# A log-sum-exp kernel: ScalarE instead of SyncE waits for the last store

## The chip, the cores and the metric

One core of a Trainium2 chip. The time is that of one execution on the device, in microseconds (us), over several executions of each kernel. Traces are of one profiled execution of each kernel. In lines of the profile PE is TensorE, ACT ScalarE, DVE VectorE, POOL GpSimd and SP SyncE; a q behind the name means that the engine's sequencer did it, and L176 is line 176 of the kernel.

## The reference

For x of shape 32 x 512 x 1024 in float32, drawn from a normal distribution, the maximum plus the logarithm of the sum of exponentials over the last axis:

```python
x_max = np.max(x, axis=axis, keepdims=True)
return (x_max.squeeze(axis) + np.log(np.sum(np.exp(x - x_max), axis=axis))).astype(np.float32)
```

The output is 16384 numbers, 64 KB; the input is 67 MB. The kernel leaves the maximum out, which this input allows.

## The kernel before

The 16384 rows lie on 128 partitions, 128 rows each. SyncE streams them in 17 chunks through a ring in the on-chip memory. ScalarE takes exponentials, and sums some rows itself; VectorE sums the rest. ScalarE takes the logarithms, the last one of 4 columns. Then SyncE stores the result and ends the program:

```python
    take_logs(late_row, NB, late[:, : NB - late_row], dves, acts)   # ScalarE's last work
    nc.sync.wait_ge(act_done, acts)
    nc.sync.dma_start(out=out_v, in_=res).then_inc(stored, 16)
    # (cut: blank lines)
    nc.sync.sem_clear(range(used[0], used[-1] + 1))   # the 19 semaphores of the run
    nc.sync.wait_ge(stored, 16)                       # the store has landed
    nc.sync.sem_inc(stored, -16)                      # its semaphore is 0 again
```

The wait and the decrement of `stored` are built into one instruction (the trace has one record of 17 ns for the two lines). The store adds 16 to its semaphore, in 16 updates from 160.984 to 161.161 us, all of them after the last of its packets had begun (160.807). Where this text says that a store or a load has landed, it means its 16th count.

The softmax here doesn't subtract the row's maximum and nothing guards it: scores larger than these inputs give would overflow.

## Time and profile before

| | before |
|---|---|
| time, median of 3 runs | 162.69 us (162.61 to 162.76) |
| span of the profiled execution (first to last instruction of the kernel) | 161.19 us |
| time of that execution | 162.52 us |
| last logarithm ends | 159.59 us |
| store issued by SyncE | 159.62 us |
| store's 16th count arrives | 161.161 us |
| SyncE's last instruction, the wait, ends | 161.194 us |

The lines of the profile behind this table stand in the prediction. In short: 159.6 us of loads, exponentials and sums, 1.6 us of store, and 1.3 us of measured time that lies outside the span. Behind the kernel's last instruction the trace has no instruction of this kernel, only updates of semaphores. Below, "the tail" means that stretch, and "the closing barrier", or "the first barrier", the first group of updates of semaphore 2 that ends in it. The "second barrier" is the group of nine updates that opens 0.79 us after the first one's end; it took 0.358 us, and is the one called undisturbed. A "hop" is the time from one such update to the next, and an engine's "own step" is the time from the end of its last recorded instruction to its first update. "On the way out" names the first five of the nine updates, and "back" the last four. These are names alone.

### The profile page before, as it was taken

What the parts mean: (1) busy time and instruction counts of PE and PEld (TensorE: products, weight loads), DVE (VectorE), ACT (ScalarE), POOL (GpSimd) and SP (SyncE); (2) the same over time, 40 slices, a digit from 0 to 9 for tenths busy, and PEclk for the clock granted to TensorE, in tenths of its full rate; (3) what the DMA queues carried; (4) which work ended last, traced back from release to release, by engine and by line L of the source; (5) the groups of instructions that cost most, each with busy time, mean ns of one, the idle gap of its engine ahead of it and who ended that gap; (6) DMA issues with size and microseconds to landing.
All of it is one profiled execution on the core that took longest, in us unless ns stands there. A gap on an engine that the chain in (4) does not pass through costs nothing.

```text
span 161.2 us, 149 instructions
## 1 busy us (share of the span) xinstructions
DVE 121.0 (75%) x46; ACT 115.1 (71%) x40; POOL 0.2 (0%) x4
## 2 busy tenths in 40 slices
DVE  0028000003999999999999699999999999999892
ACT  3170005996079960999419993999199999999995
POOL 0000000000000000000000000000000000000000
DMA  7999699899899899899889999999899999999990
GB/s 260 504 488 488 290 442 520 374 407 520 374 407 520 374 407 520 374 407 520 374 374 455 455 455 439 423 423 423 385 439 430 434 441 413 418 431 415 409 406 32
DMA packets 2592, 67.18 MB, mean 417 GB/s; under 512 B 288, under 2 KB 416, under 8 KB 928
## 3 DMA queue, kind: packets, MB, share of 16 engines
q1 hardware_dynamic: 2592, 67.18, 97.2%
HBM read 67.11 MB, written 0.07 MB: 417 GB/s over the span
## 4 chain that ended last, share of the span: by engine, by line
DMA 48%; DVE 29%; ACT 20%; issue 0%
DMA ring<-in_x_dram 48%; DVE sums L157 29%; ACT ring L137 17%; ACT ring L164 3%; ACT res L108 0%
## 5 line engine op out<-in xcount | busy, mean ns | idle before, releaser
L157 DVE TENSOR_REDUCE sums<-ring 128x8 f32<-128x8192 f32 (+5 forms) x14 | 111.2, 7994 | 37.1 <-ACT ring L137 37.0
L137 ACT ACTIVATE ring<-ring 128x8192 f32<-128x8192 f32 (+6 forms) x18 | 104.4, 5835 | 43.1 <-DMA ring<-in_x_dram 42.9
L144 DVE CUSTOM_DVE_ANT_0 ring<-ring 128x512 f32<-128x512 f32 x16 | 9.9, 686 | 0.0
L164 ACT ACTIVATE ring<-ring 128x1024 f32<-128x1024 f32 x9 | 9.3, 1042 | 0.0
L122 ACT ACT_TABLE_LOAD x1 | 1.3, 1283 | 1.4 <-PEq L70 1.4
L164 ACT ACTIVATION_READ_ACCUMULATOR ring<-ring 128x1 f32 x9 | 1.6, 174 | 0.0
L144 DVE DVE_READ_ACCUMULATOR2_ANT sums<- 128x1 f32 x16 | 1.3, 83 | 0.0
L108 ACT ACTIVATE res<-sums 128x81 f32<-128x81 f32 (+1 forms) x2 | 0.5, 248 | 0.0
L108 ACT ACTIVATE res<-late 128x4 f32<-128x4 f32 x1 | 0.2, 173 | 0.0
L209 POOL MEMSET const-bfloat16-1.0<- 128x1 bf16 x1 | 0.1, 101 | 0.0
L209 POOL MEMSET const-uint8-127<- 128x1 uint8 x1 | 0.1, 101 | 0.0
L209 POOL MEMSET const-float32-0.0<- 128x1 f32 x1 | 0.1, 98 | 0.2 <-issue 0.2
L209 POOL MEMSET const-float32-1.0<- 128x1 f32 x1 | 0.1, 98 | 0.0
## 6 DMA issues: line engine op xcount, KB each, us to landing
ring<-in_x_dram SPq DMA_DIRECT2D x1, 7680.0 KB, 24.4
ring<-in_x_dram SPq DMA_DIRECT2D x1, 7168.0 KB, 28.6
ring<-in_x_dram SPq DMA_DIRECT2D x1, 6656.0 KB, 35.7
ring<-in_x_dram SPq DMA_DIRECT2D x1, 4608.0 KB, 20.3
ring<-in_x_dram SPq DMA_DIRECT2D x2, 2048.0 KB, 16.0
ring<-in_x_dram SPq DMA_DIRECT2D x1, 3584.0 KB, 28.3
ring<-in_x_dram SPq DMA_DIRECT2D x1, 2560.0 KB, 27.3
ring<-in_x_dram SPq DMA_DIRECT2D x4, 512.0 KB, 27.0
```

The source lines that it names most:

```text
L108: nc.scalar.activation(out=res[:, lo:hi], in_=src, func=Ln).then_inc(act_done, 1)
L122: nc.scalar.preload_act_table_set("natural_log_exp_and_others")
L137: nc.scalar.activation(out=ring[:, s + lo : s + hi], in_=ring[:, s + lo : s + hi], func=Exp).then_inc(act_done, 1)
L144: nc.vector.tensor_tensor_reduce(out=ring[:, s + j, : D // 2], in0=ring[:, s + j, : D // 2], in1=ring[:, s + j, D // 2 :], scale=1.0, scal ...
L157: nc.vector.reduce_sum(out=sums[:, row + lo : row + hi], in_=ring[:, s + lo : s + hi], axis=AX).then_inc(dve_done, 1)
L164: nc.scalar.activation(out=ring[:, s + j], in_=ring[:, s + j], func=Exp, accum_out=total(row + j),).then_inc(act_done, 1)
L209: nc = _bacc.Bacc("TRN2", target_bir_lowering=False, num_devices=1)
```

## The change

The intent seems to be that SyncE, which has issued the store and cleared the semaphores, need not sit until the store has landed; ScalarE, which has nothing left to do, takes the wait.

```diff
@@ -177,8 +178,8 @@
     nc.sync.sem_clear(range(used[0], used[-1] + 1))
-    nc.sync.wait_ge(stored, 16)
-    nc.sync.sem_inc(stored, -16)
+    nc.scalar.wait_ge(stored, 16)
+    nc.scalar.sem_inc(stored, -16)
```

A blank line higher up moves all later line numbers by one: L176 of before is L177 of the changed kernel.

## The prediction

One of the limits of "the four ways", 163.3, was put down for a stall of half a microsecond, an assumption that rests on no trace of before. That the updates form a chain in a fixed order was in part assumption. That the shift passes through whole, in part 4, was an assumption too. That the semaphore writes up to 162.063 are a reset is not shown; the trace has only the writes.

> **What bounds the kernel now.** I read the page's head and chain first, then SyncE's own waits, then the tail of the timeline, then the three lines of source that the change touches, and last the single semaphore updates that the trace records after the program's end, because the change lies entirely in the last 1.6 us.
>
> ```profile
> span 161.2 us, 149 instructions
> ...
> DMA 48%; DVE 29%; ACT 20%; issue 0%
> DMA ring<-in_x_dram 48%; DVE sums L157 29%; ACT ring L137 17%; ACT ring L164 3%; ACT res L108 0%
> ```
>
> The chain that ended last is the stream of x into the ring, with the exponentials and sums that free ring rows for it. The change touches none of it. The chain view stops at the last logarithm; what follows it is this:
>
> ```profile
> 158.28 1.04 ACT L164 ACTIVATE ring<-ring 128x1024 f32<-128x1024 f32 x1
> 159.22 0.16 ACT L164 ACTIVATION_READ_ACCUMULATOR ring<-ring 128x1 f32 x1
> 159.42 0.17 ACT L108 ACTIVATE res<-late 128x4 f32<-128x4 f32 x1
> 159.62 0.35 SPq L176 DMA_DIRECT2D out_dram<-res  x1
> ```
>
> Columns: start, duration, engine, line. ScalarE's last work ends at 159.42 + 0.17 = 159.59 us; SyncE issues the store at 159.62. Then the three lines of source:
>
> ```profile
> L179 SPq EVENT_SEMAPHORE_RANGE_CLEAR  x1: 64/64/64, 160.0 to 160.0; - x1
> ```
>
> ```profile
> L181 SPq EVENT_SEMAPHORE  x1: 17/17/17, 161.2 to 161.2; - x1
> ```
>
> ```profile
> SPq L181 <- SPq L181: 1.1, 1, 1.1
> ```
>
> The first says that the clear of the 19 used semaphores is one instruction of 64 ns at 160.0. The second says that the wait and the subtraction of 16 are one instruction of 17 ns, recorded at 161.2 us, which is the span's last. The third, from SyncE's waits, says that it sat for 1.1 us first. What it sat for is the store:
>
> ```profile
> out_dram<-res SPq DMA_DIRECT2D x1, 64.0 KB, 1.5
> ```
>
> 1.5 us from issue to landing: 159.62 + 1.5 = 161.1. The trace's single semaphore updates give this finer: the 16 counts of the store arrive from 160.984 to 161.161, SyncE's instruction runs from 161.177 to 161.194, and the span ends there. The tail is set by the store's landing, not by the engine that waits for it.
>
> The measured time goes on after the span. The profiled execution took 162.52 us against a span of 161.19, so 1.33 us lie outside. The trace records no instruction of the kernel behind 161.194, but updates of semaphore 2, which the kernel doesn't use. Once the kernel runs there are: one at 1.654 us; three at 159.708, 159.747 and 159.791; five at 161.337, 161.380, 161.418, 161.453 and 161.500; then, after most other semaphores have been written once each up to 162.063, nine more from 162.287 to 162.645.
>
> [...] nine updates, and 162.645 - 162.287 = 0.358 us from first to last when nobody is late. [...] One engine was done at 1.65 (TensorE, which has no work here). The next had to be ScalarE: its update, 159.708, comes 0.119 us after ScalarE's last work ended, and the two behind it, VectorE and GpSimd, done earlier (VectorE at 158.04), posted only 39 and 44 ns after ScalarE. Then the chain stood still for 1.55 us until SyncE, the last of the five, came out of its wait: 161.337 is 0.143 us after its last instruction. Four hops back end at 161.500.
>
> [...] the last packet began at 160.807 and the last count came at 161.161, 0.35 us later. Nothing in the change shortens that.
>
> [...] the change should show as one 17 ns record that moves from SyncE to ScalarE.
>
> **The change part by part.** The built programs have the same number of instructions; nothing else changes place.
>
> 1. Removed from SyncE: one 17 ns instruction and its 1.1 us of waiting. SyncE now ends with its clear, 64 ns from 160.014, at 160.08. On the path: no. The end needs the store's 16th count at 161.161 in both programs. Gain 0.
>
> 2. Added to ScalarE: the same instruction, behind a logarithm that ended at 159.59. ScalarE has nothing else to do for 1.57 us, so no work is delayed. ScalarE's other waits of this kind are 17 ns each in the trace too (at 158.07 and 158.25). So I expect it from 161.18 to 161.19, and the span unchanged: 161.2 us. Cost 0.
>
> 3. Moved in the closing barrier: the late engine is now the second of the chain and not the fifth. Before, from the end of the late instruction: 0.143 us to SyncE's update, then 161.500 - 161.337 = 0.163 for the four hops back; together 0.306. After: 0.119 (ScalarE's figure above) to 0.143 (SyncE's, if what follows a wait costs the same on both), then all the hops from the second to the ninth update, which in the undisturbed barrier took 162.645 - 162.322 = 0.323; together 0.442 to 0.466. The difference is +0.136 to +0.160 us. It is the price of passing three further engines on the way out which before had passed while the store was in flight.
>
> 4. Does that shift reach the end? The last group of semaphores to be reset ends at 162.063, after the chain's last update, and the second barrier opens 0.224 us later. [...] the other groups end by 161.857. So the shift should pass through whole: +0.15.
>
> Sum: 162.69 + 0 + 0 + 0.15 = 162.84. I take 162.80, because I don't know where the clock of the measured time stops: if it stops at the span's end, the shift is 0, and I give that one chance in four (0.75 x 0.15 = 0.11).
>
> **The rivals.**
>
> *SyncE's ending is hidden and gains.* This is what the change seems to want: SyncE's 0.143 us between its last instruction and its update then lie beside the store. For it: they do. Against it: ScalarE has a like step (0.119), and then the chain has further to go. If ScalarE answered at once and the hops were free, the gain would be at most the 0.143: 162.55.
>
> *The program no longer waits for the store.* If only SyncE's end counted, 161.19 - 160.08 = 1.1 us would go: 161.6. Against it: the five updates at 161.337 and later came only when the last engine was free, so any engine that waits holds the rest.
>
> *ScalarE wakes or ends more slowly than SyncE.* [...] For it: TensorE's step from its last recorded instruction to its barrier update was 1.654 - 1.419 = 0.235, so engines differ. Against it: ScalarE's 0.119. At TensorE's figure the loss would be 0.235 + 0.323 - 0.306 = +0.25: 162.94. [...]
>
> *The loads change.* If an execution's ring loads shift, the time moves by some tenths either way, with either program. The three runs of before lie within 0.15 us.
>
> **The range and the chances.** The four ways span 161.6 to 163.3; the two I believe in, 162.55 to 162.94. With the spread of runs around that, 162.50 to 163.10 should hold it 8 times in 10. Two per cent are 3.25 us, over twice the 1.58 us from the store's issue to the span's end, so the whole store could vanish and the verdict would be the same. Within 2%: 0.98; 0.01 each for the sides.
>
> **What would show it right or wrong.** In the changed kernel's profile: SyncE's last record is the clear near 160.0; ScalarE has a 17 ns record near 161.18 that ends the span; the span is 161.2 within 0.15; the store takes 1.5 us from issue to landing. Step 3 is right if semaphore 2 stands at one update (TensorE's) until 161.3, and then eight follow within 0.33 us, the last 0.44 to 0.47 us after the span's end, where before it was 0.306. It is wrong if three or more of them come before the store has landed, or if the last comes no later after the span's end than before. Step 4 is wrong if the nine of the second barrier do not move with it. A span that is shorter by over 0.5 us would show that the end did not hang on the store.

## The result, and the profile after

| | before | changed |
|---|---|---|
| time, median of 4 runs of each | 162.65 us (162.58 to 162.76) | 163.01 us (162.69 to 163.12) |
| ratio | | 1.0019 (95%: 1.0001 to 1.0036) |
| span of the profiled execution | 161.19 us | 161.54 us |
| its time minus its span | 1.33 us | 1.49 us |
| from the last logarithm's end to the span's end | 1.605 us | 1.607 us |

A ratio is the mean time of one kernel's fast runs over that of the other's of the same rounds, so not quite the ratio of the medians that stand beside it.

First the page's head and chain of the changed kernel, to compare with those in the prediction:

```profile
span 161.5 us, 149 instructions
...
DMA 48%; DVE 29%; ACT 20%; issue 0%
DMA ring<-in_x_dram 48%; DVE sums L158 29%; ACT ring L138 17%; ACT ring L165 3%; ACT res L109 0%
```

The chain is the same to the per cent, and the number of instructions as well. The end of the timeline (start, duration, engine, line):

```profile
158.63 1.04 ACT L165 ACTIVATE ring<-ring 128x1024 f32<-128x1024 f32 x1
159.57 0.15 ACT L165 ACTIVATION_READ_ACCUMULATOR ring<-ring 128x1 f32 x1
159.76 0.17 ACT L109 ACTIVATE res<-late 128x4 f32<-128x4 f32 x1
159.96 0.35 SPq L177 DMA_DIRECT2D out_dram<-res  x1
```

Everything lies 0.35 us later than before, this stretch's beginning too: what made this execution's span longer was over before the change begins. Then the two lines of source that hold the clear and the wait (duration, start, engine's queue):

```profile
L180 SPq EVENT_SEMAPHORE_RANGE_CLEAR  x1: 64/64/64, 160.4 to 160.4; - x1
```

```profile
L182 ACTq EVENT_SEMAPHORE  x1: 17/17/17, 161.5 to 161.5; - x1
```

The instruction of 17 ns has moved from SPq (SyncE) to ACTq (ScalarE), and SyncE ends with the clear. SyncE's waits have lost their entry of 1.1 us; what is left of its end there is the wait ahead of the store:

```profile
SPq L177 <- ACT res L109: 29.1, 1, 29.1
```

So the plan of the change came out as written: SyncE ends 1.1 us earlier. The span's end didn't move, seen from the last logarithm, because it was the store that set it: its 16th count came at 161.502 us and the span ended at 161.540 (161.161 and 161.194 before). What moved is the tail. These are the updates of semaphore 2 from 100 us on, in us after the span's end, read from the list of updates in the two trace files (a negative number is ahead of the span's end):

```
before    first barrier   -1.486 -1.447 -1.403 | 0.143 0.186 0.224 0.259 0.306
          second barrier  1.093 1.128 1.167 1.210 1.233 1.331 1.369 1.404 1.451
changed   first barrier   0.149 0.188 0.232 0.255 0.354 0.392 0.428 0.474
          second barrier  1.261 1.295 1.334 1.378 1.401 1.499 1.538 1.572 1.619
```

One more update, at 1.65 us from the start in both, is the first of each first barrier; a full barrier has nine. Before, three more had passed 1.5 us early, and only the last engine and four hops back were left. In the changed kernel all eight come behind the store. The first barrier ends 0.474 us after the span and not 0.306, and 0.162 of these 0.168 us are hops (0.325 against 0.163); the second opens 0.787 us later in both, and its last update is 0.168 us later. Time minus span grew by 1.49 - 1.33 = 0.16 us.

The hops also show where the 0.162 us come from. In the changed kernel, as in the second barrier of both, there are 0.105 to 0.106 us from the second update to the fifth and then 0.098 (0.099 in the changed kernel's first barrier) from the fifth to the sixth. Before, with SyncE late, the step from the fifth to the sixth was 0.043. So 0.106 us are three engines more on the way out, and some 0.055 us are one hop back that is shorter when SyncE, the fifth, is the last to come. That hop was 0.043 or 0.044 in all five traces in which SyncE is last, and 0.098 or 0.099 in the seven others. Why, no run tells.

That leaves the other 0.35 us of this pair of traces, which the prediction named as a rival (the loads change) but put into no sum. The view of DMA issues (KB, us from issue to landing) shows where they began; first before, then changed:

```profile
ring<-in_x_dram SPq DMA_DIRECT2D x1, 7680.0 KB, 24.4
```

```profile
ring<-in_x_dram SPq DMA_DIRECT2D x1, 7680.0 KB, 24.7
```

This is the second chunk. The first of its 16 counts came at 25.01 us before and at 24.98 in the changed kernel, the last at 25.80 and 26.15. The first five counts came within 0.05 us of those before and the other eleven 0.26 to 0.39 us later; every later chunk then landed 0.33 to 0.36 us later than before. The page of this trace also counts one DMA packet more (2593 against 2592); the later traces of the changed kernel have 2592, so that packet does not belong to the change. Whether the change causes the lag, or chance, was the first question to the chip, for three of the changed kernel's four runs had spans of 161.5 or 161.6 us.

### The profile page after: what moved, and what is told of

The parts are those of the page before. It is cut to its first block, busy times and chain, and to the rows that moved or that the text cites. A ratio compares the mean times of both kernels' runs of the same rounds, so it can differ in the third digit from the quotient of the medians.

```text
span 161.5 us, 149 instructions
## 1 busy us (share of the span) xinstructions
DVE 121.0 (75%) x46; ACT 115.1 (71%) x40; POOL 0.2 (0%) x4
## 2 busy tenths in 40 slices
DMA packets 2593, 67.18 MB, mean 416 GB/s; under 512 B 289, under 2 KB 417, under 8 KB 929
## 3 DMA queue, kind: packets, MB, share of 16 engines
q1 hardware_dynamic: 2592, 67.18, 97.1%
## 4 chain that ended last, share of the span: by engine, by line
DMA 48%; DVE 29%; ACT 20%; issue 0%
DMA ring<-in_x_dram 48%; DVE sums L158 29%; ACT ring L138 17%; ACT ring L165 3%; ACT res L109 0%
```

## The experiments

**Theory 1**: the closing barrier is a chain with a fixed order, and a late engine costs its own step (from its last instruction to its update) plus the hops that are left behind it. **Theory 2**: the change delays the loads. **Theory 3**: the loads' tenths are chance. Rivals of theory 1 are named with each run. There were ten runs, of eight kernels, in three calls, each call on one chip with its own runs of the kernel before.

### The two kernels again

No edit.

> The kernel before, unchanged, as a control that lists the span of every run. Theory 1 (only the place of the late engine in the closing barrier counts): last update of the first closing barrier 0.306 us after the span's end, as in the first trace, and measured time minus span 1.33 us in every run. Theory 2 (the change also delays the loads, since the changed kernel's spans were 161.5, 161.2, 161.6 and 161.5): spans of this control are all near 161.2. Theory 3 (the loads' tenths are chance): this control's spans scatter from 161.2 to 161.6 as well.

> The changed kernel, unchanged. Theory 1: the barrier's last update 0.47 us after the span's end, time minus span 1.49 us in every run, so +0.16 us against the control. Theory 2: spans at 161.5 and the ratio 1.003 to 1.004 (+0.5 us). Theory 3: spans as in the control and the ratio 1.0010 (+0.16 us).

> The changed kernel once more, to pool its times and spans with the other runs of it. Theory 1: time minus span 1.48 to 1.51 us in every run against 1.31 to 1.34 of before, so +0.17 us in the time where the spans agree; the mean spans of the two kernels differ by no more than their scatter (0.2 us from run to run).

| | runs | median us | ratio to before | mean span us | time minus span us |
|---|---|---|---|---|---|
| before, beside c_before and c_after | 9 | 162.58 | | 161.30 | 1.31 |
| c_before | 5 | 162.58 | 0.9996 (0.9983 to 1.0010) | 161.20 | 1.32 |
| c_after | 5 | 162.81 | 1.0014 (1.0000 to 1.0027) | 161.30 | 1.50 |
| before, beside c_after_again | 11 | 162.32 | | 161.11 | 1.32 |
| c_after_again | 6 | 162.59 | 1.0011 (0.9995 to 1.0028) | 161.10 | 1.51 |

Theory 2 falls at the size that it was put up for, 0.3 us and more: with 25 runs of before (c_before among them) and 11 of the changed kernel on two chips, the mean spans differ by 0.04 us in the first of these calls (161.26 of before, 161.30) and by 0.01 in the other, and before alone scatters from 160.9 to 161.6. With a scatter of 0.2 us from run to run, a delay of the loads under some 0.15 us (an estimate from that scatter) could not be seen. Time minus span does not scatter: over all 36 runs of before that list it, it lies between 1.28 and 1.38 (mean 1.325; spans are listed to 0.1), over 15 of the changed kernel between 1.46 and 1.55 (mean 1.509). The two don't overlap. In the traces the first barrier ended 0.306 us after the span in c_before, 0.474 in c_after and 0.475 in c_after_again. So the change costs 0.17 to 0.18 us in the tail. The rest of the first result's 0.3 to 0.4 us did not come back in these runs, which is what theory 3 says; what makes the loads scatter is not shown.

The controls' profiles show that a span says nothing here by itself. Their heads, first c_before, then c_after:

```profile
span 161.4 us, 149 instructions
```

```profile
span 161.2 us, 149 instructions
```

Here the changed kernel had the shorter span, with times of 162.69 and 162.67 us.

### VectorE or GpSimd waits

```diff
-    nc.sync.wait_ge(stored, 16)
-    nc.sync.sem_inc(stored, -16)
+    nc.vector.wait_ge(stored, 16)      # the other run: nc.gpsimd
+    nc.vector.sem_inc(stored, -16)
```

> VectorE waits for the store. Theory 1: VectorE stands third or fourth in the chain; from an undisturbed barrier, 0.24 us (fourth) or 0.28 us (third) of hops lie behind it, and with a step of its own of 0.15 to 0.19 the last update comes 0.39 to 0.47 us after the span's end: between before and after. Rival (any engine but SyncE costs the same): 0.47, as in the changed kernel. Rival (SyncE's early end gains by itself): under 0.306.

> GpSimd waits for the store. Theory 1: as VectorE, in the other of the two places: 0.39 to 0.47 us, and semaphore 2 shows two or three updates before the store has landed and not one. If GpSimd is third and VectorE fourth, this is later than VectorE's by the 0.04 of one hop, less what the engines' own steps differ by. Rival: 0.47 whatever the engine.

Measured: VectorE 162.94 us against 162.58, ratio 1.0016 (1.0002 to 1.0029); GpSimd 163.11 us, ratio 1.0033 (1.0018 to 1.0049). The line of the wait, first with VectorE, then with GpSimd, shows the same short instruction at the span's end:

```profile
L181 DVEq EVENT_SEMAPHORE  x1: 21/21/21, 161.5 to 161.5; - x1
```

```profile
L181 POOLq EVENT_SEMAPHORE  x1: 17/17/17, 161.5 to 161.5; - x1
```

The updates of semaphore 2 from 100 us on tell them apart (us after the span's end, first barrier):

```
VectorE   -1.514 -1.475 | 0.189 0.212 0.310 0.349 0.385 0.431
GpSimd    -1.492 | 0.561 0.604 0.628 0.726 0.764 0.800 0.847
```

With the update at the start, three had passed ahead of VectorE and two ahead of GpSimd, where one had passed ahead of ScalarE and four ahead of SyncE. So the order is TensorE, ScalarE, GpSimd, VectorE, SyncE; that TensorE is the first of all is shown by its own run, the next. VectorE came out within the expectation (0.431 us). GpSimd did not: I expected at most 0.47 and got 0.847. Its hops are as expected (0.847 - 0.561 = 0.286); its own step, 0.561 us, is not, since I had put in 0.15 to 0.19 for it (0.149 was ScalarE's in the changed kernel; the 0.19 was an assumption of mine). The rival "any engine but SyncE costs the same" falls with three different numbers, "SyncE's early end gains" with all three being above 0.306. What GpSimd does in its 0.56 us, the trace doesn't say. Each of these two engines was measured in one trace.

### TensorE waits

```diff
+    nc.tensor.wait_ge(stored, 16)
+    nc.tensor.sem_inc(stored, -16)     # in place of nc.sync
```

> TensorE, first of the chain, waits for the store. Theory 1 (own step of the late engine plus the hops that are left): no update of semaphore 2 before the store has landed; TensorE's own step was 0.235 us at the program's start, all eight hops 0.358: the barrier's last update 0.59 us after the span's end, time minus span 1.31 + 0.59 - 0.306 = 1.60, that is +0.28 us on before. If the own step doesn't count (hops alone): ScalarE's measured 0.474 + 0.035 for one more hop, 0.51.

Measured: 162.68 us against 162.28, ratio 1.0018 (1.0006 to 1.0030). All nine updates came behind the store; TensorE's step was 0.279 us (expected 0.235), the eight hops 0.359, together 0.638, where 0.59 was expected. Time minus span averaged 1.68 us (expected 1.60), beside 1.34 of before on this chip. Hops alone would have given 0.51. So both terms of theory 1 are needed.

```profile
L181 PEldq EVENT_SEMAPHORE  x1: 51/51/51, 161.0 to 161.0; - x1
```

The instruction itself is longer on this engine, 51 ns against 17. That lies within the span (161.0 us here) and comes on top: from the store's 16th count to the span's end it took 0.079 us, against 0.033 with SyncE.

The five kernels with one wait, together (us):

| who waits | place | own step | hops left | first barrier ends after the span | mean time minus span |
|---|---|---|---|---|---|
| TensorE | 1 | 0.279 | 0.359 | 0.638 | 1.68 |
| ScalarE (changed) | 2 | 0.149 | 0.325 | 0.474 | 1.51 |
| GpSimd | 3 | 0.561 | 0.286 | 0.847 | 1.88 |
| VectorE | 4 | 0.189 | 0.242 | 0.431 | 1.47 |
| SyncE (before) | 5 | 0.143 | 0.163 | 0.306 | 1.33 |

The last two columns rise together: their difference is between 1.02 and 1.04 in every row. So what the first barrier takes longer, the measured time takes longer too, one for one. Where the measured clock starts and stops is not shown; time minus span is less than the 1.45 us from the span's end to the last update of semaphore 2 in the kernel before (0.31 to the first barrier's end, 0.79 to the second's opening, 0.36 for the second). At places 1 to 4 the hops left are, within 0.002 us, what an undisturbed barrier has left from that update on (0.358, 0.323, 0.284 and 0.241 us in the second barrier before); at SyncE's place that would be 0.218, and it is 0.163, by the shorter hop back.

### Both wait, and who is last?

A rival was still possible: a waiting ScalarE, or an idle SyncE, costs 0.17 us for some reason that has nothing to do with a chain. In these two kernels both engines wait for a half of the same store, and which of them waits for the later half is exchanged.

```diff
+    stored2 = nc.alloc_semaphore("stored2")
-    nc.sync.dma_start(out=out_v, in_=res).then_inc(stored, 16)
+    nc.sync.dma_start(out=out_v[:64], in_=res[:64]).then_inc(stored, 16)
+    nc.sync.dma_start(out=out_v[64:], in_=res[64:]).then_inc(stored2, 16)
     # ScalarE last; in the other kernel sync and scalar are exchanged
     nc.sync.wait_ge(stored, 16)
     nc.sync.sem_inc(stored, -16)
+    nc.scalar.wait_ge(stored2, 16)
+    nc.scalar.sem_inc(stored2, -16)
```

> The store is cut in two halves of 64 partitions, on two semaphores; SyncE waits for the first, ScalarE for the second, which lands last. Theory 1 (the last engine's place counts): last update 0.47 us after the span's end, as in the changed kernel, although SyncE waits as well. Rival (it is SyncE's early end that made the changed kernel slower): 0.306, since SyncE now waits nearly as long. The span grows by one issue, at most 0.4 us, in this run and the next alike.

> The same two halves and the same two waits, with the engines exchanged: ScalarE waits for the first half, SyncE for the second. Theory 1: ScalarE passes 0.35 us ahead of SyncE, its step of 0.149 and the hops to SyncE, 0.106, are done by then, so the last update comes 0.306 us after the span's end, as before: 0.17 us less than the run with ScalarE last, at the same store. Rival (a waiting ScalarE costs 0.17 us wherever it stands): 0.47 in both. If the halves land closer than 0.11 us apart, something in between.

Measured: 163.57 us with ScalarE last, ratio 1.0075 (1.0060 to 1.0089); 163.17 us with SyncE last, ratio 1.0052 (1.0039 to 1.0064). The waits' lines, first with ScalarE last:

```profile
L183 SPq EVENT_SEMAPHORE  x1: 17/17/17, 161.2 to 161.2; - x1
L185 ACTq EVENT_SEMAPHORE  x1: 17/17/17, 161.9 to 161.9; - x1
```

and with SyncE last:

```profile
L183 ACTq EVENT_SEMAPHORE  x1: 17/17/17, 161.5 to 161.5; - x1
L185 SPq EVENT_SEMAPHORE  x1: 17/17/17, 162.2 to 162.2; - x1
```

In each, one engine is 0.64 us behind the other. The first barrier ended 0.474 us after the span with ScalarE last and 0.304 with SyncE last; mean time minus span was 1.52 and 1.36. From the last logarithm's end to the span's end both took the same, 2.52 and 2.51 us. The updates of semaphore 2 around the end (us after the span's end, first barrier):

```
ScalarE last  0.149 0.188 0.231 0.254 0.353 0.393 0.428 0.474
SyncE last    -0.486 -0.448 -0.404 | 0.142 0.185 0.224 0.258 0.304
```

So with the same store and the same two waits, which engine is the last makes the 0.17 us. The rivals fall: ScalarE's wait costs nothing when SyncE is later, and a SyncE that waits doesn't help when ScalarE is later.

The price of the halves was a miss of mine: I expected the span to grow by one issue, at most 0.4 us. It grew by 0.9 (2.52 - 1.605). The issue lines and landings, with ScalarE last:

```profile
L177 SPq DMA_DIRECT2D out_dram<-res x1: 525/525/525, 159.4 to 159.4; - x1
```

```profile
L178 SPq DMA_DIRECT2D out_dram<-res x1: 587/587/587, 160.0 to 160.0; - x1
```

```profile
out_dram<-res SPq DMA_DIRECT2D x2, 32.0 KB, 1.9
```

A store of 64 partitions took 525 to 587 ns to issue in this run, where 128 partitions took 348, and 1.8 to 1.9 us to land where 128 took 1.5. The trace's packets show where the loss lies: the first packet of a half began 1.17 and 1.24 us after the start of its issue, that of the whole store 0.85 us after. From its first packet on, a half took 0.64 us and the whole 0.70. So the time is lost ahead of the data; why, no run here tells.

### A store in two by columns

If only what lands last counts, the store can be made small at the end, with SyncE left to wait.

```diff
             take_logs(logged, late_row, sums[:, logged:late_row], *done_before[-LATE])
+            nc.sync.wait_ge(act_done, acts)
+            nc.sync.dma_start(out=out_v[:, :late_row], in_=res[:, :late_row]).then_inc(stored, 16)
-    nc.sync.dma_start(out=out_v, in_=res).then_inc(stored, 16)
+    nc.sync.dma_start(out=out_v[:, late_row:], in_=res[:, late_row:]).then_inc(stored, 16)
-    nc.sync.wait_ge(stored, 16)
-    nc.sync.sem_inc(stored, -16)
+    nc.sync.wait_ge(stored, 32)
+    nc.sync.sem_inc(stored, -32)
```

> A try at a shorter tail, with SyncE waiting as before: the 124 columns that are ready 1.2 us earlier are stored at once, the last 4 columns after the last logarithm. Theory 1 says that only what lands last counts, so: the last update 0.306 after the span's end, and the span shorter by what a store of 4 columns lands sooner than one of 128. From the trace the packets of the whole store lie between 160.46 and 160.82, 0.36 us; what comes before (0.85 us from the issue) and after (0.35 us to the last count) is fixed. So at most 0.3 us are to be had, 0.1 us likely: ratio 0.998 to 1.000. Rival: writes of 16 bytes land more slowly than those of 512, and the time grows by 0.1 us or more.

> The split store once more. In its first profile the tail from the last logarithm's end to the span's end was 1.47 us against 1.60 of before, 0.137 less, but the runs' ratio was 1.000. If the shorter tail is real and the first result was the scatter of the loads, pooled runs tend to 0.9992 (-0.13 us) and this profile shows 1.47 again; if the early store gives back elsewhere what the tail gains, the mean span stays at that of before with the tail at 1.47.

Measured: 162.42 us against 162.28, ratio 1.0000 (0.9985 to 1.0016); again, 162.19 against 162.32, ratio 0.9991 (0.9972 to 1.0011). The timeline of the first run's tail:

```profile
158.20 0.24 ACT L108 ACTIVATE res<-sums 128x43 f32<-128x43 f32 x1
158.47 0.34 SPq L136 DMA_DIRECT2D out_dram<-res  x1
159.48 0.17 ACT L108 ACTIVATE res<-late 128x4 f32<-128x4 f32 x1
159.68 0.34 SPq L178 DMA_DIRECT2D out_dram<-res  x1
```

The first store is issued 1.2 us ahead, and had landed by 160.01. The second, 2 KB, landed 1.408 us after its issue, where the whole store took 1.546; its packets began within 0.195 us of each other, those of the whole store within 0.345. From the last logarithm's end to the span's end it took 1.468 us, and 1.466 in the second profile, against 1.605: 0.137 and 0.139 us less. The tail behind it was as in before (0.305 and 0.306). The rival of slow small writes falls. The expectation took what comes before and after the packets as fixed. That was an assumption; between these two stores of 128 partitions it held to 0.012 us, with 1.408 - 0.195 = 1.213 us here against 1.546 - 0.345 = 1.201 before, but not for the halves, whose first packet came 1.17 and 1.24 us after the start of the issue and not 0.85. The gain in the time is not shown: both intervals hold 1, and the mean spans were 161.08 beside 161.03 of before, and 161.03 beside 161.11. With spans that scatter by 0.2 us from run to run, 0.14 us can't be told from nothing by six runs. One rival was named ahead of the second run: that the early store gives back elsewhere what the tail gains. The traces leave it little room. The last chunk had landed at 158.28 us, ahead of the first store's issue at 158.47 (158.48 and 158.69 in the second profile), so that store can't have delayed a load, and from the start of the last exponential to the end of the last logarithm it took 1.303 and 1.302 us, against 1.310 before. As far as the traces go this is the better end for this kernel; as far as the times go it is the same.

## Why the prediction was right, point by point

- **The bound.** Right. The chain kept its shares, and over the later runs the mean spans agree within 0.04 us. One of the prediction's own signs failed all the same: the profiled span should have been 161.2 within 0.15 and was 161.54, by the lag of the second chunk's load.
- **Part 1, nothing gained on SyncE**, and **part 2, nothing lost on ScalarE's instruction.** Right. From the last logarithm to the span's end 1.605 us became 1.607; the moved instruction is 17 ns in both.
- **Part 3, the chain.** Right in mechanism, a little low in size: 0.136 to 0.160 us were predicted, 0.168 to 0.170 measured in three pairs of traces (the two first, c_before with c_after, and the two with halves). The hops came out at 0.325 us (0.323 predicted); the missing hundredth is ScalarE's own step, which behind a wait was 0.149 us and not 0.119 to 0.143. The reason that it gives, three further engines on the way out, is two thirds of it: they are 0.106 us, and some 0.055 are the longer hop back. The sum held because it took both sets of hops from the trace as measured. The exact order, which the trace of before left open for VectorE and GpSimd, came from the experiments.
- **Part 4, the shift reaches the end.** Right: the second barrier opens 0.787 us after the first in both. The one chance in four that the measured time stops at the span's end was misplaced; time minus span grew by 0.16 to 0.18 us. Without it the text's own sum, 162.84, is the better number.
- **The rivals.** SyncE's early end gave nothing. The program did not stop waiting for the store. TensorE's figure, which I used for a slow engine, was the right kind of caution but for the wrong engine: it is GpSimd that is slow, with 0.561 us. The loads' tenths came in the first four runs and did not come back in the later ones.
- **The number.** 162.80 was predicted, within 162.5 to 163.1, and 163.01 measured. Of the 0.2 us between, 0.06 to 0.07 belong to the change (0.17 to 0.18 us of tail, where 0.11 had been put in); the rest goes with the loads, as far as the spans tell: the first four runs had a mean span of 161.45 us, and 11 later ones, 161.2. That the range still held 163.01, above the 162.94 of the slower of the two ways that it believed in, was its allowance for scatter and not its reasoning. Later the changed kernel stood 0.23 and 0.27 us over before by medians, and 0.19 us by means in both, which is close to what the tail says.

## What to carry to other kernels

Here an engine that ended early saved nothing, because another had to wait for the same store: what counted was when the last engine got through, and how much of the end-of-program work still had to come after it. In this program that favours leaving the last wait to the engine that stands last in the closing barrier, SyncE, so that all others have passed while the store is in flight: the first barrier then ended 0.306 us after the span, and with the others 0.431 to 0.847. The gain over ScalarE, 0.17 us, is a tenth of a per cent of this kernel's time. When a change is worth a tenth or two and runs scatter by more, compare a quantity that doesn't scatter, here time minus span and the semaphore updates after the span, before asking the medians.
